# Gate units between state input units, the state gate's tile in another slot, and a state group inside the branch product

## The chip, the cores and the metric

The kernel runs on one core of one Trainium2 chip. The metric is the device time of one execution in microseconds (us). Three runs of the kernel before gave 1543.25, 1544.30 and 1544.58 us; the median is 1544.3 us.

## The reference, cut to what matters

Two layers, each a feed-forward block, a token mixer and a second feed-forward block, on 256 tokens of width 1024, all in float32. Only the mixer is touched.

```python
u = rms_norm(h, mix_norm[l])
z_s, xbc, dt_s, qkv, z_d, b_d, a_d, gate_s, gate_d = split(u @ w_in[l])
y_s = mamba2_branch(z_s, xbc, dt_s, ...)      # causal conv + silu, state-space recurrence, norm per group
y_d = deltanet_branch(qkv, z_d, b_d, a_d, ...) # conv + silu, gated delta rule, norm per head
merged = sigmoid(gate_s) * (y_s @ ssm_w_branch[l]) + sigmoid(gate_d) * (y_d @ dn_w_branch[l])
h = h + merged @ w_out[l]
```

The state branch (`mamba2_branch`) has four groups of eight heads. For each group the inputs `xs` (512 channels) go through a convolution of four taps and silu; a decay matrix of 128x128 per head and chunk of 128 tokens weighs them; the result is gated by `silu(z_s)` and normalised per group.

## The kernel before, in words

All large products run on TensorE (PE) as three products of split operands: every float32 weight tile of 128x1024 is loaded as `wraw`, rounded by ScalarE (ACT) to `whi` (line 68, `prep`), and VectorE (DVE) takes the rest, `wlo = wraw - whi` (line 71). Five raw tiles and five pairs of split tiles are kept (`NRAW`, `NSPL`), so that loads and splits run ahead of the products by five tiles; a split tile comes free when PE has made its last product with it.

The mixer is a list of units, written by hand in `ORDER`, that is gone through once per layer. The units that matter here:

- `x` g i: half of a state group's inputs (`xs_unit`). 48 products of 256 columns with two weight tiles into one PSUM bank, then for each half of the bank the convolution: ACT scales (`ca<-xs`), DVE adds three taps (`ca<-xs,lp,ca`), ACT applies silu into `xsT` (`xsT<-ca`).
- `g` s n p: half of a gate's product (`gate`), for s=0 the state gate and s=1 the delta gate. 24 products of 512 columns with two weight tiles; two halves fill two PSUM banks, and ACT takes tanh of them into the tile `tg` (`tg<-t`).
- `D` g: the decay of group g (`decay`). SyncE's queue (SP) loads 1 MB from DRAM into the tile `dc`; DVE subtracts (`dc<-dc,ac`), limits (`dc<-dc`, line 78), ACT takes exp, DVE multiplies (`dc<-dc,cbt`). Even groups have `dc` in slot `sA`, odd ones in `sB`; a group's load starts when PE has made the last `ydb` product of two groups before.
- `S` g and `T` g: the two halves of `ssd`. `S` transposes `xsT` on PE into two banks `xsb` (eight transposes, four chunks of channels by two halves of the tokens), and DVE makes `xD`, `xdt` and `xe` of them. `T` multiplies with the decay (`ydb`, 32 pairs of products, and `yob`), DVE adds and gates (`xD`, `yo`, `yz`), ACT sums the squares (`jk`), GpSimd (POOL) takes the reciprocal root (`srr`, line 210), and ACT scales (`yz<-yz,srr`).
- `o`, `N`: the delta branch's product (`dn_T`, `dn_branch`): PE transposes a head pair (`oT`), DVE multiplies (`og`), ACT and DVE split it (`bh<-og`, `bl<-og`), then PE makes 24 products `b` of 512 columns per pair, 96 in all, over four PSUM banks.
- `y` and, after the list, `branch("s", 8, ss_T)`: the state branch's product; eight pieces of 24 products `b`, for each of which PE transposes `yz` (`yT`) and ACT and DVE split it (`bh<-yT`, `bl<-yT`) one piece ahead.

The list sets each unit's weights in the order of loading and the order in which tiles and banks are handed out. Within that, a scheduler orders the instructions of each engine; each engine then runs its own list strictly in turn, so an instruction that waits holds up all behind it. PSUM has four banks for products (`accb`) and four for transposes and small products (`trb`), each handed out in turn. A slot such as `sC` holds one tile at a time: first `Q`, then `BC` (the state branch's B and C), which the `cbb` products read for the last time before the first gate unit ends. The state gate's tile `tg` shares `sA` with the decays of groups 0 and 2.

Of the kernel before, what the change touches and what calls it, by code (L numbers as in the profile page):

```python
# [7 lines left out]
F32 = mybir.dt.float32  # L8
# [8 lines left out]
P = 128  # L17
D = 1024
# [26 lines left out]

ORDER = """
z20 s z10 z11 s z21 s M k1 k0 q1 k2 k3 K1 K0 q3 q0 K3 K2 v0 q2 I Q0 I Q3 I z30 v1 z31 Q2 v2 V0 I v3
V1 I V3 I Q1 V2 d0 R R R b3 R b2 b0 R b1 R d2 R x00 R d1 x01 R d3 R R P R g100 g101 D0 S0 x10 T0 D1
x11 g110 g111 S1 x20 T1 o x21 N D2 y S2 D3 x30 x31 T2 g000 g010 g001 S3 g011 T3
""".split()  # L50


# [1 line left out]
def trunk_kernel(ctx, tc, x, wst, wsm, norms, lpar, rpar, cst, out):  # L54
# [5 lines left out]
    slots = ctx.enter_context(tc.tile_pool(name="slots", bufs=1))  # L60
# [6 lines left out]
    def act(o, i, func=AF.Copy, **kw):  # L67
        return A.activation(out=o, in_=i, func=func, **kw)  # L68
# [21 lines left out]
    def accb(name):  # L90
        return accp.tile([P, 512], F32, tag="acc", name=name)
# [9 lines left out]
    def plan_plain(j, n):  # L101
        for i in range(j, j + n):
            stream.append(("w", i))
            plan.append(("d", [len(stream) - 1], len(stream)))
        return j + n

    def plan_ffn(j):


        o, j2, held = j + 4 * FC, j + 4 * FC + 22, []  # L110
        for kind in FFN:
            if kind in "fc":
                j = plan_plain(j, 4 if kind == "f" else 2)
            elif kind == "d":
                o = plan_plain(o, 1)
            elif kind == "A":
                y = len(stream)
                stream.extend([("y", o), ("w", o + 1), ("w", o + 2)])
                plan.append(("q0", (y, y, y + 1), y + 2))
                plan.append(("q1", (y, y + 1, y + 2), y + 3))  # L120
                plan.append(("q2", (y + 1, y, y + 2), y + 3))
                plan.append(("q3", (y, o + 3), y + 3))
                held.append((y, o + 2))
                o += 4
            else:
                y, b22 = held.pop(0)
                stream.append(("w", b22))
                plan.append(("q4", (len(stream) - 1,), len(stream)))
                stream.append(("w", b22 + 1))
                plan.append(("q5", (len(stream) - 1,), len(stream)))  # L130
                plan.append(("q6", (y,), len(stream)))
        return j2

    j0 = 0
    for _ in range(DEPTH):
        j0 = plan_ffn(plan_plain(plan_ffn(j0), mix))
# [259 lines left out]
    def out_chunks(ps, stat, ks, last, group=1, split=False, first=None):  # L396

        for g0 in range(0, len(ks), group):
            kk = ks[g0 : g0 + group]
            ws = [(k, take()) for k in kk]  # L400
            for t in range(2):
                order = [(k, n) for n in range(2) for k in range(len(kk))]
                if t == 1 and not split:
                    m = len(kk) - 2 if len(kk) == NSPL else len(kk)
                    order = [(k, n) for k in range(m) for n in range(2)]
                    order += [(k, n) for n in range(2) for k in range(m, len(kk))]
                order = [(k, n, 0, 512) for k, n in order]
                if t == 1 and split:
                    order = [o for o in order if o[1] == 0]
                    order += [(k, 1, c, c + 256) for c in (0, 256) for k in range(len(kk))]  # L410
                state["sums"] = []
                for k, n, c0, c1 in order:
                    k, (wh, wl) = ws[k]
                    sh, sl = stat(k, t)
                    c = slice(n * 512 + c0, n * 512 + c1)
                    begin = k == 0 if first is None else first and t == n == 1
                    bank = ps[t][n][:, c0:c1]
                    if c0:
                        begin, bank = k == kk[0], ps[2][:, 0:256]
                    ins = mm3(bank, sh, sl, wh[:, c], wl[:, c], begin, k == last)  # L420
                    state["sums"].append(ins)
# [171 lines left out]
    def mixer(l, nxt):  # L593
# [17 lines left out]
        def tok_unit(key, part, done):  # L611

            if part != 1:
                open_[key] = [accb("t0"), accb("t1")]
            tok_chunk(open_[key], range(KT) if part is None else range(4 * part, 4 * part + 4))
            if part != 0:
                for t in range(2):
                    done(t, open_[key][t])

        def z_unit(g, part):  # L620
            if part != 1:
                yz[g] = slots.tile([P, 2, 512], F32, tag=f"y{g}", name="yz")
            tok_unit(("z", g), part, lambda t, ps: act(yz[g][:, t, :], ps[:], AF.Silu))
# [386 lines left out]
        def drain(g):  # L1010
            for _ in g:
                pass
# [15 lines left out]
        def bcm(i):  # L1028
            if "BC" not in late:
                late["BC"] = slots.tile([P, 8, S], F32, tag="sC", name="BC")  # L1030
            bc_unit(i, late["BC"])

        def zdm(i):
            if "zdT" not in late:
                late["zdT"] = slots.tile([P, 8, S], F32, tag="sE", name="zdT")
            zd_unit(i)
# [102 lines left out]
        tg = {}  # L1139

        def gate(s_, n, part):
            if s_ not in tg:
                tg[s_] = slots.tile([P, 2, D], F32, tag=("sA", "sD")[s_], name="tg")
            v = tg[s_][:, :, n * 512 : (n + 1) * 512]
            tok_unit(("g", s_, n), part, lambda t, ps: act(v[:, t, :], ps[:], AF.Tanh, scale=0.5))

# [28 lines left out]
                stt(ol[:, k], bank[:, k * S : (k + 1) * S], w, f(oh[:, k]), ALU.mult, ALU.subtract)  # L1175
            brT[("s", j)] = (oh, ol)

        def branch(kind, n, mk, tail=1):
            ps = [[accb("b"), accb("b")] for _ in range(2)]
            held = {}  # L1180

            def stat(k, t):
                oh, ol = held[k // 2]
                return oh[:, k % 2, t * P : (t + 1) * P], ol[:, k % 2, t * P : (t + 1) * P]

            made = 1
            for j0 in list(range(n - tail)) + [n - tail]:
                js = range(j0, j0 + (tail if j0 == n - tail else 1))
                while made < min(js[-1] + 2, n):
                    mk(made)  # L1190
                    made += 1
                for j in js:
                    held[j] = brT.pop((kind, j))
                out_chunks(ps, stat, [2 * j + i for j in js for i in range(2)], 2 * n - 1, group=2 * len(js))
            return ps

        def dn_branch():
            ps = branch("d", 4, dn_T)
            m = tg[1]
            for t in range(2):  # L1200
                for n in range(2):
                    sl = slice(n * 512, (n + 1) * 512)
                    stt(m[:, t, sl], m[:, t, sl], 1.0, ps[t][n][:], ALU.add, ALU.mult)
# [5 lines left out]
        def step(name):  # L1209
            kind, arg = name[0], name[1:]  # L1210
            num = [int(c) for c in arg if c.isdigit()]
            if kind == "z":
                z_unit(num[0], num[1])
            elif kind in "kqv":
                rests[name] = units[kind](*num)
            elif kind in "KQV":
                drain(rests[name.lower()])
            elif kind == "s":
                next(sc, None)
            elif kind == "M":  # L1220
                masks()
            elif kind == "I":
                next(inv, None)
            elif kind == "R":
                next(rc, None)
            elif kind == "b":
                bcm(*num)
            elif kind == "d":
                zdm(*num)
            elif kind == "x":  # L1230
                xs_unit(*num)
            elif kind == "P":
                drain(ssd_pre())
            elif kind == "D":
                decay(*num)
            elif kind == "g":
                gate(*num)
            elif kind == "S":
                heads[num[0]] = ssd(*num)
                next(heads[num[0]])  # L1240
            elif kind == "T":
                drain(heads[num[0]])
            elif kind == "o":
                dn_T(0)
            elif kind == "y":
                ss_T(0)
            elif kind == "N":
                dn_branch()
# [1 line left out]
        for name in ORDER:  # L1250
            step(name)
        m = tg[1]
        ps = branch("s", 8, ss_T)
        mh = slots.tile([P, KT, S], F32R, tag="sE", name="mh")
        ml = slots.tile([P, KT, S], F32R, tag="sH", name="ml")
        def merge(t):
# [30 lines left out]
    for t in range(2):  # L1287
# [3 lines left out]
        o = tmp2("fo"), tmp2("fo")  # L1291
        for i, (c0, c1) in enumerate(cuts):
            junk = tmp2("junk")
            act(junk[:, : c1 - c0], h[:, t, c0:c1], AF.Square, scale=1.0 / 32.0, accum_out=ss[:, i : i + 1])
            n = c0 // 512
# [143 lines left out]
```

## Time and profile before

| | |
|---|---|
| time, median of three runs | 1544.3 us |
| span of the profiled execution | 1539.7 us |
| median less that span | 4.6 us |
| PE, busy share of the span | 99% |
| DVE | 80% |
| ACT | 61% |
| mixer's part from the first gate unit to the merge, layer 1 and 2 | about 400 to 569 us and 1160 to 1330 us |

The profile is of one execution; of it the span alone is told, and the 4.6 us that it lacks against the median lie before its first and after its last instruction, or are the difference between two executions. The views used below are the page (shares and the chain of waits that ended last), groups of instructions with their mean time, the instructions in order of time, and busy time by stretches. "x24" is a count; a bracket at a row's end tells how long the engine sat idle before it and what ended that.

### The profile page before, as it was taken

How to read it: one execution, taken by the hardware profiler on the slowest of the kernel's cores; microseconds unless marked ns; L12 is line 12 of the kernel's file. 1: busy time of each engine (PE TensorE's matmuls, PEld its weight loads, DVE VectorE, ACT ScalarE, POOL GpSimd, SP SyncE). 2: the span in 40 equal slices, each digit the busy share in tenths (PEclk: the TensorE clock that was granted, in tenths of full speed). 3: DMA queues.
4: the chain of work that ended last, by engine and by line, in shares of the span. 5: the costliest groups of instructions: out<-in, count | busy, mean ns of one | idle time of the engine just before them, and what ended most of it. 6: DMA issues, size and time to landing. Idle time of an engine off the chain costs nothing.

```text
span 1539.7 us, 29072 instructions
## 1 busy us (share of the span) xinstructions
PE 1522.8 (99%) x11473; PEld 1384.4 (90%) x11473; DVE 1229.7 (80%) x1859; ACT 944.8 (61%) x1532; POOL 81.8 (5%) x92
## 2 busy tenths in 40 slices
PE   8999999999999999999999999999999999999998
PEld 7999889999888888999899998899998888899997
DVE  6878769967899766789778887689589996677886
ACT  5655667765665645555555566676756666455565
POOL 0000110000000000000100012010000000000010
PEclk9999999999999999999999999999999999999999
DMA  7687775653565556587867687665345555556785
GB/s 277 190 265 231 226 228 167 187 164 111 178 213 171 163 166 196 185 256 211 261 225 225 208 253 229 197 193 180 117 141 202 179 170 186 176 177 195 247 241 156
DMA packets 98831, 305.73 MB, mean 199 GB/s; under 512 B 22837, under 2 KB 23813, under 8 KB 97670
## 3 DMA queue, kind: packets, MB, share of 16 engines
q1 hardware_dynamic: 93796, 290.95, 57.2%
q0 software_dynamic: 4608, 12.58, 5.1%
q8 instruction: 90, 1.47, 0.4%
q14 instruction: 47, 0.39, 0.1%
q10 hardware_dynamic: 290, 0.33, 0.1%
HBM read 297.72 MB, written 1.92 MB: 195 GB/s over the span
## 4 chain that ended last, share of the span: by engine, by line
PE 89%; DVE 4%; ACT 2%; DMA 2%; issue 1%; SPq 1%; POOL 0%; POOLq 0%; ACTq 0%; DVEq 0%
PE fc L346 10%; PE fc L340 9%; PE fc L345 9%; PE t L366 9%; PE o L337 4%; PE o L335 4%; PE o L336 4%; PE f L366 3%; PE b L335 3%; PE b L337 3%; PE b L336 3%; PE p L336 2%; PE p L337 2%; PE p L335 2%; PE xs L345 1%; PE xs L340 1%
## 5 line engine op out<-in xcount | busy, mean ns | idle before, releaser
L71 DVE TENSOR_TENSOR wlo<-wraw,whi 128x1024 fp32r<-128x1024 f32 x488 | 591.8, 1221 | 186.7 <-ACT whi L68 172.2
L68 ACT ACTIVATE whi<-wraw 128x1024 fp32r<-128x1024 f32 x488 | 511.6, 1059 | 271.0 <-PE fc L345 92.5
L346 PE MATMUL fc<-uW,wlo 128*128 128x256 f32 x1280 | 354.9, 277 | 0.0
L340 PE MATMUL fc<-uW,whi 128*128 128x256 f32 x1280 | 354.1, 277 | 0.0
L345 PE MATMUL fc<-uW,whi 128*128 128x256 f32 x1260 | 348.3, 276 | 0.0
L340 PEld LDWEIGHTS fc<-uW,whi 128*128 128x128 f32 x1280 | 240.5, 188 | 0.8
L346 PEld LDWEIGHTS fc<-uW,wlo 128*128 128x128 f32 x1280 | 240.5, 188 | 0.0
L345 PEld LDWEIGHTS fc<-uW,whi 128*128 128x128 f32 x1260 | 236.5, 188 | 0.8
L366 PE MATMUL t<-whi,uW 128*128 128x512 f32 x512 | 165.3, 397 | 0.0
L366 PEld LDWEIGHTS t<-whi,uW 128*128 128x128 f32 x512 | 95.9, 188 | 21.6 <-issue 1.3
L68 ACT ACTIVATE whi<-wsum 128x1024 fp32r<-128x1024 f32 x64 | 68.0, 1062 | 58.8 <-PE fc L345 32.9
L366 PE MATMUL t<-wlo,uW 128*128 128x512 f32 x256 | 100.2, 392 | 0.0
L71 DVE TENSOR_TENSOR wlo<-wsum,whi 128x1024 fp32r<-128x1024 f32 x64 | 78.2, 1221 | 7.9 <-ACT whi L68 5.6
L335 PE MATMUL b<-whi,bh 128*128 128x512 f32 x192 | 76.1, 398 | 0.3
L336 PE MATMUL b<-wlo,bh 128*128 128x512 f32 x192 | 74.9, 390 | 0.0
L337 PE MATMUL b<-whi,bl 128*128 128x512 f32 x192 | 74.2, 393 | 0.0
L340 PE MATMUL xs<-uW,whi 128*128 128x256 f32 x256 | 72.8, 284 | 0.0
L346 PE MATMUL xs<-uW,wlo 128*128 128x256 f32 x256 | 71.4, 279 | 0.0
L345 PE MATMUL xs<-uW,whi 128*128 128x256 f32 x254 | 70.6, 278 | 0.0
L335 PE MATMUL o<-whi,gh 128*128 128x512 f32 (+1 forms) x160 | 62.0, 388 | 0.0
L337 PE MATMUL o<-whi,gl 128*128 128x512 f32 (+1 forms) x160 | 61.8, 386 | 0.0
L336 PE MATMUL o<-wlo,gh 128*128 128x512 f32 (+1 forms) x160 | 61.7, 386 | 0.0
(337 smaller groups left out, 3291.7 us busy)
## 6 DMA issues: line engine op xcount, KB each, us to landing
wraw<-in_wst_dram SPq DMA_DIRECT2D x504, 512.0 KB, 4.9
wsum<-in_wst_dram SPq DMA_DIRECT2D x16, 512.0 KB, 7.3
wsum<-in_wst_dram POOLq DMA_DIRECT2D x16, 512.0 KB, 8.7
dc<-rdram SPq DMA_DIRECT2D x8, 1024.0 KB, 8.5
nw<-in_norms_dram SPq DMA_DIRECT2D x6, 512.0 KB, 5.9
h<-u POOLq DMA_DIRECT2D x12, 256.0 KB, 6.8
gb<-rdram SPq DMA_DIRECT2D x8, 256.0 KB, 5.6
h<-in_x_dram SPq DMA_DIRECT2D x4, 256.0 KB, 3.7
```

Source lines behind the costliest of these rows:

```text
L68: return A.activation(out=o, in_=i, func=func, **kw)
L71: return V.tensor_tensor(out=o, in0=a, in1=b, op=op)
L335: PE.matmul(ps, lh, rh, start=start, stop=False)
L336: PE.matmul(ps, lh, rl, start=False, stop=False)
L337: return PE.matmul(ps, ll, rh, start=False, stop=stop)
L340: PE.matmul(ps, wh, mh, start=start, stop=False)
L345: PE.matmul(ps, wh, ml, start=False, stop=False)
L346: PE.matmul(ps, wl, mh, start=False, stop=stop)
L366: ins = PE.matmul(ps[t][:], st, mv, start=k0 == 0 and j == 0, stop=k0 == KT - 2 and j == 5)
```

## The change

Three edits of the mixer. In `ORDER` the gate units no longer stand in blocks: one half of a gate unit stands between two `x` units, and the decays `D2` and `D3` and the halves `T1`, `T2` move with them. `S3` and `T3` leave the list and are called inside the state branch's product, before its pieces 1 and 3 (`between`). The state gate's tile moves from slot `sA` to `sC`, so that the first half of that gate can stand before the decay of group 2 has been used.

```diff
@@ ORDER @@
-V1 I V3 I Q1 V2 d0 R R R b3 R b2 b0 R b1 R d2 R x00 R d1 x01 R d3 R R P R g100 g101 D0 S0 x10 T0 D1
-x11 g110 g111 S1 x20 T1 o x21 N D2 y S2 D3 x30 x31 T2 g000 g010 g001 S3 g011 T3
+V1 I V3 I Q1 V2 d0 R R R b3 R b2 b0 R b1 R d2 R x00 R d1 x01 R d3 R R P R g100 D0 g101 S0 x10 T0 D1
+g110 x11 g111 S1 g000 x20 g001 T1 D2 o x21 N y S2 x30 D3 g010 T2 x31 g011
@@ gate @@
-                tg[s_] = slots.tile([P, 2, D], F32, tag=("sA", "sD")[s_], name="tg")
+                tg[s_] = slots.tile([P, 2, D], F32, tag=("sC", "sD")[s_], name="tg")
@@ branch @@
-        def branch(kind, n, mk, tail=1):
+        def branch(kind, n, mk, tail=1, between={}):
...
             for j0 in list(range(n - tail)) + [n - tail]:
                 js = range(j0, j0 + (tail if j0 == n - tail else 1))
+                if j0 in between:
+                    step(between[j0])
                 while made < min(js[-1] + 2, n):
@@ after the list @@
-        ps = branch("s", 8, ss_T)
+        ps = branch("s", 8, ss_T, between={1: "S3", 3: "T3"})
```

The instructions are the same in number on every engine; their order moves. Up to group 0's `ydb` it is the same on PE, DVE, ACT and SP. Three places, the same in both layers:

PE, group 1's transposes `xsb`. Before, six of the eight follow `g111`, and the last two stand 15 products into `x20`:

```order
L340 MATMUL xs<-uW,whi 128x256
L345 MATMUL xs<-uW,whi 128x256
L1101 MATMUL xsb<-cs,xsT 128x128 x2
L346 MATMUL xs<-uW,wlo 128x256
L340 MATMUL xs<-uW,whi 128x256
```

In the change four follow `g111`, two stand seven products into `g000`, and the last two eight products into `x20`:

```order
L342 MATMUL xs<-uW,whi 128x128
L343 MATMUL xs<-uW,whi 128x128
L346 MATMUL xs<-uW,wlo 128x256
L340 MATMUL xs<-uW,whi 128x256
L1101 MATMUL xsb<-cs,xsT 128x128 x2
L345 MATMUL xs<-uW,whi 128x256
```

Both read the `xsT` of `x11`. Between the end of `x11` and the last two there stood `g110`, `g111` and 15 products; now there stand `g111`, `g000` and eight products, and `x11` itself comes 24 products later.

ACT, after group 1's `ydb` (`jk`, `yz`) and at the start of the delta branch's product (`bh<-og`). Before:

```order
L68 ACTIVATE jk,sss<-yz 128x512
L68 ACTIVATE whi<-wraw 128x1024
L68 ACTIVATE jk,sss<-yz 128x512
L68 ACTIVATE ca<-xs,lp 128x256
L68 ACTIVATE bh<-og 128x512
L68 ACTIVATE xsT<-ca 128x256
L68 ACTIVATE yz<-yz,srr 128x512 x2
```

The change:

```order
L68 ACTIVATE xsT<-ca 128x256
L68 ACTIVATE jk,sss<-yz 128x512 x2
L68 ACTIVATE whi<-wraw 128x1024
L68 ACTIVATE yz<-yz,srr 128x512 x2
L68 ACTIVATE bh<-og 128x512
L68 ACTIVATE ca<-xs,lp 128x256
```

The first `bh`, which the branch's first product reads, now stands behind the two `yz` that need POOL's `srr`.

DVE, the same place. Before:

```order
L71 TENSOR_TENSOR yz<-yz,xD 128x512
L74 SCALAR_TENSOR_TENSOR ca<-xs,lp,ca 128x254
L74 SCALAR_TENSOR_TENSOR og<-oT,lp,zdT 128x512
L74 SCALAR_TENSOR_TENSOR ca<-xs,lp,ca 128x253
L79 TENSOR_SCALAR sss<-sss 128x2
L71 TENSOR_TENSOR wlo<-wraw,whi 128x1024
L71 TENSOR_TENSOR bl<-og,bh 128x512
```

The change:

```order
L71 TENSOR_TENSOR yz<-yz,xD 128x512
L74 SCALAR_TENSOR_TENSOR og<-oT,lp,zdT 128x512
L79 TENSOR_SCALAR sss<-sss 128x2
L71 TENSOR_TENSOR dc<-dc,ac 128x2048
L71 TENSOR_TENSOR wlo<-wraw,whi 128x1024
L71 TENSOR_TENSOR bl<-og,bh 128x512
```

The subtraction of group 3's decay, which needs that group's load, now stands before the first `bl`; before, it stood after the fourth `og`. On SP the load of group 3's decay moves behind four more weight tiles.

## The prediction, on record before the changed kernel ran

> **What bounds the kernel now.** I read the page's shares first, then the chain of waits, then the stretches of the first layer's mixer.
>
> ```profile
> PE 1522.8 (99%) x11473; PEld 1384.4 (90%) x11473; DVE 1229.7 (80%) x1859; ACT 944.8 (61%) x1532; POOL 81.8 (5%) x92
> PE 89%; DVE 4%; ACT 2%; DMA 2%; issue 1%; SPq 1%; POOL 0%; POOLq 0%; ACTq 0%; DVEq 0%
> core 0: us, PE busy (x) PEld busy (x) DVE busy (x) ACT busy (x) POOL busy (x), PEclk, DMA share, GB/s
> 424.30:459.40 35.10, 34.06 (x283) 30.64 (x281) 34.40 (x51) 24.89 (x38) 2.35 (x2) 1.00 0.68 221
> 459.40:482.20 22.80, 22.76 (x103) 18.70 (x104) 21.58 (x27) 12.63 (x17) 0.87 (x1) 1.00 0.46 138
> 482.20:523.30 41.10, 41.10 (x345) 35.40 (x344) 36.33 (x50) 26.28 (x36) 1.60 (x1) 1.00 0.56 187
> 523.30:569.00 45.70, 45.70 (x216) 37.62 (x215) 28.16 (x38) 23.39 (x35) 0.70 (x1) 1.00 0.53 170
> ```
>
> PE is busy 99% of the span, at a clock of 1.00 in these stretches. No product is removed, so the change can win only the time in which PE waits. The four stretches show where that is: from group 0's `ydb` to the delta branch's product, 35.10 us of which DVE works 34.40, PE lacks 1.04 us; in the other three it lacks 0.04 us at most. DVE is full at the front (34.40 of 35.10) and loose at the back (28.16 of 45.70); the change moves gate products, which ask little of DVE, forward, and group 3's work back. Its aim is the 1.04 us. A busy PE may still run below its pace, so I looked at starts in order of time:
>
> ```profile
> 497.13 16.54 PE t L366 x72
> 385.55 0.28 PE L340 MATMUL xs<-uW,whi 128*128 128x256 f32 x1
> 385.66 0.28 PE L345 MATMUL xs<-uW,whi 128*128 128x256 f32 x1
> 443.38 0.28 PE L345 MATMUL xs<-uW,whi 128*128 128x256 f32 x1
> 444.59 0.44 PE L1101 MATMUL xsb<-cs,xsT 128*128 128x128 f32 x2 [0.93 <-ACT xsT L68]
> 1205.95 0.33 PE L1101 MATMUL xsb<-cs,xsT 128*128 128x128 f32 x1 [0.94 <-ACT xsT L68]
> 458.25 1.04 PE L1154 MATMUL oT<-cs,vb 128*128 128x128 f32 x8
> 459.44 0.50 PE L335 MATMUL b<-whi,bh 128*128 128x512 f32 x1
> ```
>
> A product of 512 columns takes 16.54/72 = 0.23 us, so 24 take 5.5; one of 256 columns about 0.115 us, so a unit of 48 takes 5.6. Starts further apart than that, where the change works, are two in each layer: 1.1 us (443.38 to 444.59, less one product) before group 1's last two transposes, which wait for `xsT`; and about 0.4 us before the delta branch's first product, for `bh`. That is all that can be won: 1.5 us a layer, 3.0 us in all, 0.19% of 1544.3. A change of 0.2%, 3.1 us, is about what a measurement of this kernel tells from none.
>
> **The change part by part.** PE's work is the same; the transposes stand in other pieces. Group 1's are in three pieces instead of two, but `oT` loses one (ten and two become twelve) and group 3's stand next to `yT`. The two transposes at 444.59 held PE for 0.2 us beyond the wait, so one piece less is worth about 0.1 us a layer; bounds 0 to 0.2.
>
> *Group 1's last transposes (gain).* They need the second half of `x11` through the convolution. In the change `x11` runs after `g110` (5.5 us later, ends at about 435.8), then come `g111` to 441.2, six transposes and `g000` to 447.7, eight products to 448.7. On ACT stand before that `xsT`: two tanh, which wait for `g111` (441.4), `whi`, `xsT` and `ca`, then group 2's exp between two table loads.
>
> ```profile
> 453.71 1.28 ACT L68 ACT_TABLE_LOAD   x1
> 455.01 0.42 ACT L68 ACTIVATE xsT<-ca 128x256 f32<-128x256 f32 x1
> L68 ACT ACTIVATE dc<-dc 128x2048 f32<-128x2048 f32 x8 | 15.3, 1916 | 0.1
> L68 ACT ACTIVATE whi<-wraw 128x1024 fp32r<-128x1024 f32 x488 | 511.6, 1059 | 271.0 <-PE fc L345 92.5 <-DMA wraw<-in_wst_dram 29.1 <-PE b L337 27.7
> ```
>
> From 441.4: 0.5 (tanh) + 1.0 (`whi`) + 0.4 + 0.5 (`xsT`, `ca`) + 1.3 + 1.9 + 1.3 + 0.4 = 7.3, so `xsT` is there at 448.7, when PE is. The wait of 1.1 falls to about 0.2: 0.9 us won a layer. There is no slack in it: 1 us late on ACT and nothing is won. Bounds 0 to 1.1.
>
> By the Trainium skill ("ScalarE: Activation LUTs", section "What ACT_TABLE_LOAD costs") each switch of tables costs a load of about 1.28 us and a drain of about 1.38 more. The rows agree with the first and not with the second: the load of 453.71 is followed by `xsT` 1.30 us later. By the page's whole price the two loads ahead of `xsT` would put it 2.8 us later, an estimate from its figures.
>
> *The delta branch's first product (loss).* Take S for the start of group 1's `ydb`.
>
> ```profile
> 449.04 2.02 PE ydb L1115 x64
> 456.32 0.68 DVE L71 TENSOR_TENSOR yz<-yz,xD 128x512 f32<-128x512 f32 x1
> 458.41 0.17 DVE L79 TENSOR_SCALAR sss<-sss 128x2 f32<-128x2 f32 x1
> 458.66 1.61 POOL L210 TENSOR_TENSOR srr<-sss,mhalf 128x2 f32<-128x2 f32 x1 [25.77 <-DVE sss L79]
> 458.76 0.62 ACT L68 ACTIVATE bh<-og 128x512 fp32r<-128x512 f32 x1
> 460.30 1.34 ACT L68 ACTIVATE yz<-yz,srr 128x512 f32<-128x512 f32 x2 [0.61 <-POOL srr L210]
> ```
>
> Before, `bh` went at S+9.7, ahead of `yz`. In the change the convolution of `x20` has run through by then (`g001` lies between), so the last `yz` product on DVE is about 1.2 us earlier (S+6.1 for S+7.3) and `sss` comes at S+7.7. But `bh` now stands behind both `yz`, which stand behind POOL: S+7.7, 0.25 to POOL's start, 1.61, then 1.34, then 0.62 for `bh` itself: S+11.5. PE is there at S+10.35 (before, 459.08 = S+10.05 without its wait, and two transposes more ahead). PE waits 1.15 us where it waited 0.4: 0.75 us lost a layer. Behind `bh` on ACT wait the `ca` of `x21` and the next `whi`, both with room. Bounds: 0.4 won (POOL's result in time) to 1.2 lost.
>
> *Group 3's decay (a load in front of the first `bl`).* Its load cannot start before group 1's `ydb` has ended:
>
> ```profile
> 451.09 0.33 SPq L1061 DMA_DIRECT2D dc<-rdram  x1
> DMA to landing us min/median/max: 6.2/8.5/10.6
> 470.05 2.28 DVE L71 TENSOR_TENSOR dc<-dc,ac 128x2048 f32<-128x2048 f32 x1
> L71 DVE TENSOR_TENSOR wlo<-wraw,whi 128x1024 fp32r<-128x1024 f32 x488 | 591.8, 1221 | 186.7 <-ACT whi L68 172.2 <-PE wb L891 4.0
> 459.63 0.68 DVE L71 TENSOR_TENSOR bl<-og,bh 128x512 fp32r<-128x512 f32 x1
> ```
>
> Issued at S+2.1 it lands at S+8.3 to S+12.7; DVE wanted it at S+21 before and reaches it at S+7.8 now. Behind it stand one `wlo` and the first `bl`: 2.25 + 1.15 + 0.65 = 4.05 us from landing to the end of `bl`. PE can make six products with `bh` alone (1.4 us), so it needs `bl` at S+12.9, and the load must land by S+8.85, 6.7 us after its issue. The load of 451.09 took 6.5 us, the one in its place in layer 2 6.2. I take that, as there too one weight tile was under way beside it: nothing lost. Bounds 0 to 1.8 (the median of 8.5), and 3.9 at the maximum.
>
> *Group 3 in the state branch.* `S3` adds five operations of 0.6 us to DVE and `T3` six, in a stretch of 45.70 us where DVE has 17.5 us free; PE's pieces last 5.9 us each and the splits run five tiles ahead. What stands closest:
>
> ```profile
> 529.24 0.48 PE L335 MATMUL b<-whi,bh 128*128 128x512 f32 x1
> 529.26 0.46 ACT L68 ACTIVATE bh<-yT,lp 128x256 fp32r<-128x256 f32 x1
> 529.75 0.48 DVE L74 SCALAR_TENSOR_TENSOR bl<-yT,lp,bh 128x256 fp32r<-128x256 f32 x1 [1.93 <-ACT bh L68]
> 530.49 0.40 PE L337 MATMUL b<-whi,bl 128*128 128x512 f32 x1
> ```
>
> The piece after `T3` had its second `bl` ready at 530.23 and used it at 530.49, before; the same sequence now falls at piece 4, with one `wlo` less in between. Nothing lost; up to 0.5 if the 0.26 us go. The fourth bank of the branch comes free with the convolution of `x31`, now one gate half (5.5 us) before the branch instead of four (both halves of `g00`, of `g01`): I put the last tap about 4 us after `g011` and PE's first use there too, 0.1 us lost, bounds 0 to 0.5. If either cover goes, PE stands still for as long.
>
> *Slot.* `sC` is free when `g000` comes (its `cbb` readers end by about 405, `g000` starts at 441), so the tile makes no wait: 0.
>
> Sum for a layer: -0.1 - 0.9 + 0.75 + 0 + 0 + 0.1 = -0.15 us; two layers, -0.3 us. The profiled span goes from 1539.7 to 1539.4; the runs lay 4.6 us above that span, and I keep that: 1544.3 - 0.3 = **1544.0 us**, no change that can be told.
>
> **Rivals.**
> 1. *All waits go.* For it: two gate halves move in ahead of the delta branch, 11 us of PE with 4.9 us of splits for DVE. Against: group 3's subtraction now needs a load before S+8.85, and `bh` stands behind POOL. 2 x (1.1 + 0.4 + 0.1) = 3.2: 1541.1 us.
> 2. *Slower: the decay's load holds DVE in front of the first `bl`.* One mechanism, at the start of the delta branch's product: it decides from 6.7 us between issue and landing on. For it: the median of the eight such loads is 8.5. Against: the two at this place took 6.5 and 6.2. At 8.5 us 1.8 us a layer, with the sum above 2 x 1.65 = 3.3: 1547.6 us; at the maximum of 10.6, 1552.
> 3. *Table switches on the way to `xsT`.* Two loads and exp now stand before group 1's last `xsT`, where before they came after it. Were each switch to hold ACT as long again as its load (1.28 us), `xsT` would come 2.6 us later and PE wait for it: 2 x (2.6 - 0.15) = 4.9, 1549.2 us. Against: 1.30 us from load to next start in the trace. (This is the page's rule named above, with its price of a switch; by the page's own drain it is 2.8 for 2.6.)
>
> That the change does not do what it says is not among them: the order on PE and DVE shows the units moved.
>
> **How the numbers follow.** Forecast 0.74; rival 1 0.07; rival 2 0.16; rival 3 0.03. Rival 1 ends at the edge of 3.1 us, so faster takes 0.05 of it and 0.01 from the forecast's own spread; slower takes rivals 2 and 3 and 0.02 of the spread, 0.21. The forecast's own range, 1541.8 to 1546.8, holds one of its terms at its bound per layer (a loss of 1.2 for 0.75, or `xsT` late by 1). The range reaches up to rival 2's price and some of its tail: 1541.2 to 1548.6 us.
>
> **What would show it.** Right: PE's wait before group 1's last transposes under 0.5 us, released by ACT `xsT`; before the first `b` a wait of about 1 us released by ACT `bh`, with `yz` before it waiting for POOL; group 3's `dc<-dc,ac` within 1 us after its load's landing at about S+8.5. In the state branch no start later than its pace. Wrong: a wait of DVE for `dc` over 1 us and PE waiting for `bl`; PE idle in the branch before piece 1, 4 or 6; any stretch outside the mixer that moves.

## The result and the profile after

The changed kernel takes 1546.22 us (median of 18 runs, 1544.04 to 1551.44), the kernel before 1543.22 us on the same chips (18 runs, 1541.56 to 1544.79): a ratio of 1.0022, with a 95% interval of 1.0015 to 1.0029. On another chip, in the fourth experiment below, it was 1.0013 (1.0004 to 1.0022). The change makes the kernel about 2 to 3 us slower; the forecast was no change, 1544.0 us. The profiled execution took 1545.48 us with a span of 1543.7, 4.0 us over the span before.

The page of the changed kernel, its shares and its chain of waits:

```profile
PE 1524.5 (99%) x11473; PEld 1384.4 (90%) x11473; DVE 1230.9 (80%) x1859; ACT 945.1 (61%) x1532; POOL 78.2 (5%) x92
PE 89%; DVE 3%; DMA 3%; ACT 3%; issue 2%; SPq 1%; POOL 0%; POOLq 0%; ACTq 0%
```

Nothing shows there: the sums are nearly those of before. What moved stands in the view of PE's waits over one mixer (engine, line, what it waited for: us in total, times, longest). First the kernel before, the row before the fourth `cbb` in the first and the second layer (the ones for `xsb` <- `xsT`, 0.9 us each, are the two that the prediction showed in the timeline):

```profile
PE cbb L1045 <- DVE vb L71: 0.6, 1, 0.6
...
PE cbb L1045 <- DVE vb L71: 1.3, 1, 1.3
```

The same view of the changed kernel, first and second layer:

```profile
PE b L337 <- DVE bl L71: 1.0, 1, 1.0
PE cbb L1045 <- DVE vb L71: 0.9, 1, 0.9
PE b L335 <- ACT bh L68: 0.3, 1, 0.3
...
PE cbb L1045 <- DVE vb L71: 1.9, 1, 1.9
PE b L337 <- DVE bl L71: 1.3, 1, 1.3
PE b L335 <- ACT bh L68: 0.3, 1, 0.3
```

The wait for `xsT`, 0.9 us a layer, is gone, as forecast. In its place stands a wait for the first `bl` of the delta branch, 1.0 and 1.3 us. The view counts from the modelled end of the product before; by starts, as the prediction counts, each wait is about 0.2 us longer. The rows of the timeline in the first layer, and of the two starts in the second:

```profile
461.79 0.33 SPq L1061 DMA_DIRECT2D dc<-rdram  x1
467.40 0.17 DVE L79 TENSOR_SCALAR sss<-sss 128x2 f32<-128x2 f32 x1
467.65 0.69 POOL L210 TENSOR_TENSOR srr<-sss,mhalf 128x2 f32<-128x2 f32 x1 [34.30 <-DVE sss L79]
468.38 1.34 ACT L68 ACTIVATE yz<-yz,srr 128x512 f32<-128x512 f32 x2
468.88 2.29 DVE L71 TENSOR_TENSOR dc<-dc,ac 128x2048 f32<-128x2048 f32 x1 [1.31 <-DMA dc<-rdram]
469.62 0.62 ACT L68 ACTIVATE bh<-og 128x512 fp32r<-128x512 f32 x1
470.29 0.51 PE L335 MATMUL b<-whi,bh 128*128 128x512 f32 x1 [0.27 <-ACT bh L68]
...
471.58 0.39 PE L336 MATMUL b<-wlo,bh 128*128 128x512 f32 x1
472.23 0.68 DVE L71 TENSOR_TENSOR bl<-og,bh 128x512 fp32r<-128x512 f32 x1
472.97 0.50 PE L337 MATMUL b<-whi,bl 128*128 128x512 f32 x1 [1.00 <-DVE bl L71]
...
1232.65 2.29 DVE L71 TENSOR_TENSOR dc<-dc,ac 128x2048 f32<-128x2048 f32 x1 [1.58 <-DMA dc<-rdram]
1235.07 0.39 PE L336 MATMUL b<-wlo,bh 128*128 128x512 f32 x1
1236.73 0.50 PE L337 MATMUL b<-whi,bl 128*128 128x512 f32 x1 [1.27 <-DVE bl L71]
```

Group 3's decay load was issued at 461.79 and landed at 468.86, 7.07 us later. DVE stood idle for it for 1.31 us, then came the subtraction, one `wlo` and `bl`. PE made its six products with `bh` and waited from 471.81 (471.58 + 0.23) to 472.97: 1.16 us; in the second layer 1236.73 - 1235.07 - 0.23 = 1.43. This is the second rival of the prediction. But POOL's `srr` took 0.69 us and not 1.61, so `bh` was there at 470.2 and PE lost only 0.49 us ahead of it (0.36 before).

The waits before the fourth `cbb` (0.6 and 1.3 before, 0.9 and 1.9 after) lie ahead of all that the change moves, on a stretch with the same order in both kernels. They come back below, since they vary between executions by as much as the whole effect.

### The profile page after: what moved, and what is told of

Same layout as the page of the kernel before. It is cut to its first block, busy times and chain, and to the rows that moved or that the text cites. A ratio compares the mean times of both kernels' runs of the same rounds, so it can differ in the third digit from the quotient of the medians.

```text
span 1543.7 us, 29056 instructions
## 1 busy us (share of the span) xinstructions
PE 1524.5 (99%) x11473; PEld 1384.4 (90%) x11473; DVE 1230.9 (80%) x1859; ACT 945.1 (61%) x1532; POOL 78.2 (5%) x92
## 3 DMA queue, kind: packets, MB, share of 16 engines
HBM read 297.72 MB, written 1.92 MB: 194 GB/s over the span
## 4 chain that ended last, share of the span: by engine, by line
PE 89%; DVE 3%; DMA 3%; ACT 3%; issue 2%; SPq 1%; POOL 0%; POOLq 0%; ACTq 0%
PE t L366 10%; PE fc L346 9%; PE fc L340 9%; PE fc L345 9%; PE o L337 4%; PE o L335 4%; PE o L336 4%; PE f L366 3%; PE b L337 3%; PE b L335 3%; PE b L336 3%; DMA dc<-rdram 2%; PE p L336 2%; PE p L337 2%; PE p L335 2%
```

## The experiments

All were compared with the kernel before on the same chip. The lists of waits are the view shown above, of the first layer unless said otherwise.

**1. Group 3's subtraction behind the last `og`.** The one edit to the changed kernel:

```
+    with tc.issue_after(last_og):        # group 3 only
         tt(dc, dc, ac..., ALU.subtract)
```

> The changed kernel with one edit: group 3's subtraction (dc<-dc,ac) may issue on DVE only behind the last og of the delta branch, so the first bl no longer stands behind the decay's load. Theory (the load holds DVE, DVE holds bl, PE waits 1.16 and 1.43 us for it): PE's wait before the first b<-whi,bl goes to under 0.2 us in both layers, the time falls by about 2.6 us against the changed kernel, to about 1543.6 us, ratio to the kernel before 0.999 to 1.001. Rival (bh behind the yz scaling): bl still stands behind bh, nothing changes, ratio 1.002. Rival (group 3's work inside the state branch): nothing changes before that branch, ratio 1.002. Rival (the new order of gate and state input units as such): ratio 1.002.

Measured: 1542.95 us, ratio 0.9996 (0.9987 to 1.0005). The load took 7.08 us, as before the edit. PE's waits in the branch and ahead of it (0.5 for 0.6 in the second layer):

```profile
PE cbb L1046 <- DVE vb L71: 0.6, 1, 0.6
...
PE b L335 <- ACT bh L68: 0.3, 1, 0.3
```

The wait for `bl` is gone and the time with it: 2.3 us under the changed kernel on the same chip (1545.25, the fourth). The units, the slot and the state branch's groups stand as in the change, so what the change loses hangs on the place of this subtraction. With it the rest of group 3's decay (minimum, exp and multiply) comes later too, and PE takes the first `bl` products earlier in its list. Whether the loss comes through the load that the subtraction waits for, or through its own 2.29 us, this run doesn't say: it takes both away.

**2. `bh` ahead of group 1's `yz` on ACT.**

```
     rsqrt(rr, ss)
+    yield                                # after sss and srr
     for t in range(2): act(yv, yv, scale=rr[:, t])
 ...
 elif kind == "o":
     dn_T(0)
+    with tc.issue_after(first_bh): drain(heads[1])
```

> The changed kernel with one edit: on ACT the two yz scalings of group 1 stand behind the first bh instead of ahead of it. Theory (decay's load): PE's wait before the first b (0.49 us) goes to about 0.1, but it gains nothing, since the first bl still comes when the decay's load has landed and PE's wait there grows by what the first b gained; time as the changed kernel's within 0.4 us, ratio to the kernel before 1.002. Rival (bh behind yz is what costs): the time falls by 1 us or more, ratio 1.0015 or lower.

Measured: 1545.26 us, ratio 1.0011 (1.0002 to 1.002), the changed kernel's time (1545.25). PE's wait in the branch, first layer:

```profile
PE b L337 <- DVE bl L71: 1.2, 1, 1.2
```

The wait for `bh` is gone, the one for `bl` is 0.1 to 0.2 us longer, and the time is the same. The edit moved more than ACT: the scheduler put one `wlo` behind the first `bl` on DVE, and eight of the twelve `oT` ahead of the first product behind it on PE, so that PE and `bl` both come more than 1 us earlier after group 1's `ydb`. No gain from an earlier `bh` can be told while the decay's load holds `bl`.

**3. The kernel before, with group 3's decay early.**

```
-x11 g110 g111 S1 x20 T1 o x21 N D2 y S2 D3 x30 ...
+x11 g110 g111 S1 x20 T1 D3 o x21 N D2 y S2 x30 ...
```

> The kernel before with one edit: group 3's decay stands directly behind the end of group 1 in the list, so that its subtraction, which needs a load that cannot start before group 1's ydb has ended, stands on DVE ahead of the delta branch's first og and bl. None of the change's other edits is in it. Theory (decay's load holds DVE): a new wait of DVE for dc and of PE in the delta branch's first piece, 1 to 4 us a layer (og is held too, so bh as well), time 2 to 8 us over the kernel before, ratio 1.0013 to 1.005. Rivals (bh behind yz; group 3 in the state branch; the new order of the units): none of these is in this kernel, ratio 1.000.

Measured: 1561.52 us, ratio 1.0115 (1.0101 to 1.0129): 18 us, far more than any theory gave. It doesn't bear out the load:

```profile
459.11 2.29 DVE L71 TENSOR_TENSOR dc<-dc,ac 128x2048 f32<-128x2048 f32 x1 [0.19 <-DMA dc<-rdram]
...
464.93 1.28 ACT L68 ACT_TABLE_LOAD   x1
466.22 1.91 ACT L68 ACTIVATE dc<-dc 128x2048 f32<-128x2048 f32 x1
468.04 0.61 ACT L68 ACTIVATE bh<-og 128x512 fp32r<-128x512 f32 x1
468.70 0.80 PE L335 MATMUL b<-whi,bh 128*128 128x512 f32 x1 [4.34 <-ACT bh L68]
```

The load (6.46 us) landed as DVE came to it. With the decay that early the scheduler also put its minimum on DVE ahead of `og`, and its table load and exp on ACT ahead of the first `bh`. PE waited for `bh`. The kernel shows how dear this place is for anything else, and tells nothing on the load.

**4. The changed kernel once more**, on the chip of the first three.

> The changed kernel itself, on the same chip and in the same rounds as the other three, so that their differences against it can be read. Ratio to the kernel before 1.002 (1.0015 to 1.0029 the first time). In its profile PE's wait for the first bl, 1.16 and 1.43 us the first time, comes again at 0.8 to 1.8 us a layer if it is the decay's load, which took 7.1 to 7.3 us there and decides from 6.7 us.

Measured: 1545.25 us, ratio 1.0013 (1.0004 to 1.0022). The waits, first layer and second:

```profile
PE cbb L1045 <- DVE vb L71: 1.8, 1, 1.8
PE b L337 <- DVE bl L71: 0.8, 1, 0.8
...
PE cbb L1045 <- DVE vb L71: 1.9, 1, 1.9
PE b L337 <- DVE bl L71: 1.4, 1, 1.4
```

The wait for `bl` came again; here the load took 6.81 us in the first layer, and DVE waited 1.07. The wait before `cbb` tripled against the profile before (0.6), in a stretch where nothing differs.

**5. The first two edits together.**

> Both edits in the changed kernel: group 3's subtraction behind the last og on DVE, and group 1's yz scalings behind the first bh on ACT. Theory (the decay's load gates the first bl, and bh behind yz is the next wait, 0.49 us a layer, which counts only once the load is out of the way): PE's waits before the first b and the first bl are both under 0.15 us, the time is 0.8 us under that of the kernel with the first edit alone (2 x 0.4), ratio to the kernel before 0.9985 to 0.9998. If the first bh gains nothing even so: the same ratio as that kernel, 0.9996.

Measured: 1542.6 us, ratio 0.9997 (0.9988 to 1.0006). On PE eight `oT` move as in the second. No wait is left in the branch, but the 0.8 us against the first experiment can't be told: in the second layer of its profile PE waited 2.4 us before `cbb`, where it was 0.5 in the first experiment's. A gain of that size is below what these runs tell apart.

**6. Group 3 out of the state branch again.**

```
-x30 D3 g010 T2 x31 g011
+x30 D3 x31 T2 g010 S3 g011 T3            # and no between in branch("s", ...)
```

> The changed kernel with its part for the state branch undone: S3 and T3 stand in the list again, T3 ahead of the branch, x31 ahead of T2; all else as changed, the decay's load included. The prediction's term for group 3 in the state branch (0, and 0.1 us for the bank of x31): the ratio stays at 1.0013 to 1.002, PE's wait for the first bl stays at 0.9 to 1.6 us. Rival (group 3's work in the branch costs what the change lost): ratio back to 1.000.

Measured: 1544.83 us, ratio 1.0009 (1.0000 to 1.0018), with the wait for `bl` in place:

```profile
PE b L337 <- DVE bl L71: 1.2, 1, 1.2
```

Undoing this part leaves the wait. The time alone decides little: the interval touches 1.0000 and overlaps the changed kernel's, so a cost of some tenths of a us, as the prediction had for the bank of `x31`, is not excluded.

**9. The decay's load ahead of a weight load.** In the changed kernel three weight loads of 0.5 MB had been issued in the 6 us ahead of the decay's; the edit puts the last of them behind it on SP's queue, and leaves the order of every other engine (a tie behind the first `og`, not shown in the cut, keeps the subtraction in its place):

```
+    T1 L3 D2 ...                          # L3: group 3's load alone
+    if state.get("decay"):                # in load(): the next weight tile
+        behind.enter_context(tc.issue_after(state.pop("decay").ins))
```

> The changed kernel with one edit: on SP's queue the weight load that stood just ahead of group 3's decay load stands behind it; the order on PE, DVE, ACT and POOL is the changed kernel's, group 3's subtraction ahead of the first bl included. In the changed kernel three weight loads of 0.5 MB were issued in the 6 us ahead of the decay's (456.08, 457.65, 460.74 us, against 461.79) and it took 7.07 us; in the kernel before one was, and it took 6.46. Theory (the first bl waits for the subtraction because the load lands late, and the load is late for the weight loads in flight): the load takes 5.5 to 6.4 us, DVE's wait for it goes from 1.3 to under 0.5 us, PE's wait for the first bl from 1.2 to 1.6 us to 0.2 to 0.7, time 1 to 2 us under the changed kernel's, ratio 1.0000 to 1.001. Rival (it is the subtraction's own 2.3 us on DVE ahead of bl, not the load): PE's wait stays over 1 us, ratio 1.0013 to 1.002.

Measured: 1547.15 us, ratio 1.0026 (1.0016 to 1.0036): not better. In the first layer the load was as late as ever (issued 463.08, DVE started at 470.12), with the weight load issued right behind it. In the second it took 5.3 us (1226.43 to 1231.73), and that layer is the telling one:

```profile
470.12 2.29 DVE L71 TENSOR_TENSOR dc<-dc,ac 128x2048 f32<-128x2048 f32 x1 [1.24 <-DMA dc<-rdram]
...
1232.12 2.29 DVE L71 TENSOR_TENSOR dc<-dc,ac 128x2048 f32<-128x2048 f32 x1
1232.30 2.67 POOL L212 TENSOR_TENSOR srr<-sss,mhalf 128x2 f32<-128x2 f32 x1 [34.49 <-DVE sss L79]
1236.91 0.50 PE L337 MATMUL b<-whi,bh 128*128 128x512 f32 x1 [2.24 <-ACT bh L68]
```

DVE didn't wait for the load, and PE lost more than ever. The subtraction ran at once, just ahead of POOL's `srr`, which took 2.67 us for the 0.69 of the changed kernel; `yz` and `bh` stood behind it. The theory of the load alone fell here.

**12. Half of the load.** To see that apart from the weight loads, group 3's load was cut to 0.5 MB, with the orders of PE, DVE and ACT as in the changed kernel (the same tie as in the ninth; on POOL a memset of 0.95 us comes in, done 4.9 us ahead of `srr`). The decay of the group's other four heads is left out of the computation:

```
+    n = 4 if g == 3 else 8
-    dma_start(dc[:], rdram[8 * g : 8 * g + 8]...)
+    dma_start(dc[:, 0:n], rdram[8 * g : 8 * g + n]...)
+    if n < 8: G.memset(dc[:, n:8], 0.0)
```

> The changed kernel with group 3's decay load cut to its first four heads (0.5 MB for 1 MB; the other four heads are set to zero on POOL, so that half of group 3's decay is left out of the computation). The order on PE, DVE, ACT and SP is the changed kernel's: the subtraction of 2.29 us still stands ahead of the first bl. Theory (it is the landing of the load): the load takes 5 to 6 us instead of 7.0, DVE's wait for it (1.07 to 1.71 us in the profiles of the changed kernel) is under 0.4 us, PE's wait for the first bl (0.94 to 1.58 us, 0.13 to 0.15 us under DVE's wait each time) goes under 0.25 us, and the time falls by about 2 us to that of the kernel before, ratio 0.9995 to 1.0008. Rival (the subtraction's own 2.29 us of DVE ahead of bl): PE's wait stays over 0.9 us, ratio 1.0013 to 1.002.

Measured: 1547.4 us, ratio 1.0024 (1.0012 to 1.0035). Both the theory and its rival missed: the wait for `bl` went, the time didn't fall.

```profile
467.15 2.29 DVE L71 TENSOR_TENSOR dc<-dc,ac 128x2048 f32<-128x2048 f32 x1
467.32 2.68 POOL L210 TENSOR_TENSOR srr<-sss,mhalf 128x2 f32<-128x2 f32 x1 [4.88 <-DVE sss L79]
470.03 1.33 ACT L68 ACTIVATE yz<-yz,srr 128x512 f32<-128x512 f32 x2 [2.03 <-POOL srr L210]
471.27 0.61 ACT L68 ACTIVATE bh<-og 128x512 fp32r<-128x512 f32 x1
471.94 0.50 PE L335 MATMUL b<-whi,bh 128*128 128x512 f32 x1 [2.25 <-ACT bh L68]
```

The load took 5.51 us and DVE didn't wait. The subtraction held POOL's `srr`, that held `yz`, `yz` held `bh`, and PE waited 2.47 us (by starts) ahead of the first `b`, 2.61 in the second layer, where the changed kernel loses 0.49 + 1.16 and 0.49 + 1.43.

**13. Half of the load, and `bh` ahead of `yz`** (the edits of the twelfth and the second).

> The kernel of the twelfth experiment (half of group 3's decay load, so half of its decay left out; orders of the engines as changed) with the edit of the second: group 1's yz scalings behind the first bh on ACT. In the twelfth PE waited 2.47 and 2.61 us for the first bh, which stood behind yz and so behind POOL's srr, 2.68 and 2.83 us long there against 0.69 in the changed kernel, while DVE ran the subtraction of 2.29 us. Theory (DVE's subtraction holds POOL's srr, srr holds yz, yz holds bh): srr stays at 2.7 us, but bh no longer stands behind it, so PE's wait before the first b goes under 0.2 us, the first bl (not held by the load either) under 0.3, and the time falls by 4 to 5 us against the twelfth, ratio 0.9990 to 1.0005. Rival (bh is late by itself, or its og is): PE's wait before the first b stays over 1.5 us, ratio 1.002.

Measured: 1543.0 us, ratio 1.0002 (0.9993 to 1.0011).

```profile
469.07 2.68 POOL L210 TENSOR_TENSOR srr<-sss,mhalf 128x2 f32<-128x2 f32 x1 [4.88 <-DVE sss L79]
469.65 0.61 ACT L68 ACTIVATE bh<-og 128x512 fp32r<-128x512 f32 x1
470.32 0.49 PE L335 MATMUL b<-whi,bh 128*128 128x512 f32 x1
471.78 1.34 ACT L68 ACTIVATE yz<-yz,srr 128x512 f32<-128x512 f32 x2 [1.51 <-POOL srr L210]
```

`srr` is as long as in the twelfth, but `bh` no longer stands behind it: neither the first `b` nor the first `bl` waits. With that the chain from DVE's subtraction over POOL to `bh` is shown. That `bl` doesn't wait either owes something to the scheduler, which here, as in the second, put the `wlo` of 1.22 us behind it.

**7, 8, 10 and 11. The wait before the fourth `cbb`.** It has the same form: on DVE `vb` and the `cbm` multiplies stand behind group 0's subtraction, which waits for its load. Four kernels tried to win it.

```
 7 (before):  subtractions of groups 0 and 1 behind the last cbm multiply
10 (before):  group 1's decay load six weight loads later
 8 (changed): as 7, with the edits of 1 and 2
11 (changed): as 10, with the edits of 1 and 2
```

> The kernel before with one edit: the subtractions of groups 0 and 1 may issue on DVE only behind the last cbm multiply, so that the cbm multiplies and with them the banks of cbb no longer stand behind a decay's load. It tests the same mechanism at its other place, which both kernels have: PE's wait before the fourth cbb, 0.85 and 1.53 us before (0.79 to 2.14 in the runs so far, with a load of 8.5 to 11.3 us). Theory: that wait goes, 2.0 to 2.4 us, ratio 0.9985. Against it: DVE is busy 34.40 of 35.10 us from group 0's ydb on, and the subtraction that comes later may be late for group 0's ydb; then the wait stands there instead and the ratio is 1.000.

> The changed kernel with all three edits: group 3's subtraction behind the last og, group 1's yz scalings behind the first bh, the subtractions of groups 0 and 1 behind the last cbm multiply. If the waits add up: 1545.3 - 2.6 (first bl) - 0.8 (first bh) - 2.2 to 4 (fourth cbb, 2.07 and 2.14 us in the second profile of the changed kernel) = 1538 to 1540 us, ratio to the kernel before 0.9965 to 0.998. If the front's wait only moves to group 0's ydb: 1542, ratio 0.999.

> The kernel before with one edit: group 1's decay load, which is issued 1.5 us after group 0's, is issued six weight loads later; its subtraction then stands on DVE behind group 0's ydb. Group 0's load lands after 8 to 9 us, with 1 MB of group 1's behind it in the same queue. Theory (the transfers in flight share the 16 DMA engines, so the second load delays the first): group 0's load lands 1 us or more earlier, PE's wait before the fourth cbb goes from 0.85 to 2.1 us to under 0.4, and the time falls by 1 to 2.5 us if nothing is late for it later, ratio 0.9985 to 0.9995. Rival (the load is served in order, the second does not touch the first): the wait stays, ratio 1.000.

> The changed kernel with group 3's subtraction behind the last og, group 1's yz scalings behind the first bh, and group 1's decay load six weight loads later: the fifth experiment (ratio 0.9997) with the edit of the tenth. If the front's wait goes in both layers (0.28 and 2.68 us in the fifth experiment's profile): 1.5 to 3 us under the kernel before, ratio 0.998 to 0.999, faster than both kernels. If the second load does not delay the first: 0.9997.

Measured: the seventh 1544.28 us, ratio 1.0007 (0.9998 to 1.0017); the eighth 1548.07, 1.0032 (1.0020 to 1.0044); the tenth 1543.02, 0.9995 (0.9986 to 1.0004); the eleventh 1551.41, 1.0053 (1.0040 to 1.0066). Where the wait went, a row or more of each in the order 7, 8, 10, 11 (PE's waits, for the eighth also POOL, ACT and DVE, for the eleventh POOL):

```profile
PE xsb L1105 <- ACT xsT L68: 1.3, 1, 1.3
...
PE xsb L1105 <- ACT xsT L68: 3.0, 1, 3.0
434.66 4.94 POOL L210 TENSOR_TENSOR srr<-sss,mhalf 128x2 f32<-128x2 f32 x1 [27.71 <-DVE sss L79]
439.63 1.34 ACT L68 ACTIVATE yz<-yz,srr 128x512 f32<-128x512 f32 x2 [4.62 <-POOL srr L210]
441.95 1.23 DVE L71 TENSOR_TENSOR wlo<-wraw,whi 128x1024 fp32r<-128x1024 f32 x1 [2.91 <-ACT whi L68]
...
PE cbb L1045 <- DVE vb L71: 0.6, 1, 0.6
...
PE t L366 <- ACT whi L68: 2.6, 1, 2.6
PE cbb L1046 <- DVE vb L71: 1.2, 1, 1.2
437.33 8.28 POOL L210 TENSOR_TENSOR srr<-sss,mhalf 128x2 f32<-128x2 f32 x1 [27.35 <-DVE sss L79]
```

In the seventh and eighth the wait for `cbb` is gone, and a longer one for `xsT` stands later in the same stretch, where DVE had 0.7 us to spare before (the prediction's 34.40 of 35.10 us); what delays `xsT` in the seventh was not followed further. In the eighth the rows show the chain of the twelfth at another place: two `wlo` and group 2's subtraction ran one after another on DVE (434.48 to 439.04), group 0's `srr` took 4.94 us, `yz` and the `whi` behind it waited on ACT, DVE then waited for `whi`, and the last tap ahead of `xsT` came late. In the tenth the wait for `cbb` stayed (0.6 and 1.6 us): group 1's load, which in the first layer follows 1.5 us behind, is not what makes group 0's late. In the eleventh five operations ran in a row on DVE (two `wlo` and three of the decays, 437.16 to 445.06), group 0's `srr` took 8.28 us in both layers, and PE waited for the `whi` behind it, 2.6 us in the first layer and 1.0 in the second. No run takes this chain apart in the eighth and eleventh; it is read from their rows. None is told faster than the kernel before.

## Why the prediction was wrong

**The step that failed** is the term for group 3's decay: "I take that [6.5 us] ... nothing lost. Bounds 0 to 1.8". It was 1.16 and 1.43 us in the two layers, 0.94 and 1.58 in the second profile. Two things were wrong in it.

First the duration. The loads in that place took 6.5 and 6.2 us before, with one weight load issued 0.6 us ahead and the one before that 5.9 us ahead. In the changed kernel the three last ones were issued 5.7, 4.1 and 1.1 us ahead, of which the second landed 1.7 us after the decay's issue, and the decay's load took 7.07, 6.81, 7.08 and 7.03 us in the first layer of the changed kernel, its repeat, the first and the second experiment. The move of the gate units forward also moved their weight tiles' loads, and the step looked at the queue's order only, not at what is in flight. That the weight loads cause the difference is an argument, not shown. For it: in the seventh experiment the last weight load stood 5.7 us ahead in both layers, and the decay's took 4.7 and 4.5 us. Against: taking the last one from ahead of it in the ninth left the load at 7.0 us in one layer and gave 5.3 in the other.

Second, and more, the term was not independent of the one before it. The limit of 6.7 us was worked out for a PE that is held until S+11.5 by `bh`. With DVE idle in wait for the load, POOL's `srr` ran in 0.69 us, `bh` came 0.9 us earlier and PE asked for `bl` about 0.75 us earlier (S+12.15 for S+12.9, S being the start of group 1's `ydb`): the limit was then 467.72 - 461.79 = 5.9 us (PE wants `bl` at 471.81, 1.16 us before it starts; so the landing would have to be 1.16 us ahead of DVE's start at 468.88). And a load that has landed when DVE comes to the subtraction lets it start ahead of `srr`, which makes `bh` late:

| kernel, layer | DVE waits for the load | `srr` | PE waits for `bh` | for `bl` | together |
|---|---|---|---|---|---|
| changed, 1 | 1.31 | 0.69 | 0.49 | 1.16 | 1.65 |
| changed, 2 | 1.58 | 0.70 | 0.49 | 1.43 | 1.92 |
| ninth, 1 | 1.24 | 0.70 | 0.49 | 1.12 | 1.61 |
| ninth, 2 | 0 | 2.67 | 2.46 | 0 | 2.46 |
| twelfth, 1 | 0 | 2.68 | 2.47 | 0 | 2.47 |
| twelfth, 2 | 0 | 2.83 | 2.61 | 0 | 2.61 |
| first (subtraction later), 1 | - | 0.70 | 0.49 | 0 | 0.49 |
| before, 1 | - | 1.61 | 0.36 | 0 | 0.36 |

Late or early, with the subtraction in that place and `bh` behind `yz` one of the two waits stood in every layer measured. Where DVE waits for the load, PE's wait for `bl` is 0.12 to 0.15 us less than DVE's, in each of these rows.

**Point by point.** *Group 1's last transposes*: right; the wait went from 1.09 to 0.29 and 0.30 us (0.2 forecast), with `xsT` done at 449.07 (448.65 + 0.42; 448.7 forecast). *Table switches* (third rival): out. In the changed kernel's timeline the second load is followed 1.30 us after its start, as the first is (444.12, exp at 445.42):

```profile
447.35 1.28 ACT L68 ACT_TABLE_LOAD   x1
448.65 0.42 ACT L68 ACTIVATE xsT<-ca 128x256 f32<-128x256 f32 x1
```

The drain that the Trainium skill gives ("ScalarE: Activation LUTs", "What ACT_TABLE_LOAD costs") on top of the load doesn't show here either.

*The delta branch's first product*: the order was right, `bh` behind `yz` behind `srr`, and `sss` came at S+7.74 (S = 459.66; S+7.7 forecast). The size was wrong: 0.13 us lost for 0.75, through `srr`, 0.69 us for the 1.61 taken from a row in which DVE had run a `wlo` beside it. *Group 3 in the state branch*: no new wait in the view; undoing it changed nothing that can be told. *Bank of `x31`*: the starts of the branch's first piece lie 0.16 us further behind their pace than before (0.25 for 0.09), 0.1 forecast. *Slot*: no wait at `g000` shows.

**The sum.** By starts and for both layers: transposes -1.6, first `b` +0.3, first `bl` +2.6, first piece of the branch +0.3: +1.6 us, where the forecast's terms gave -0.3. Of the 4.0 us between the two profiled spans another 0.95 is the `cbb` wait, 0.34 + 0.61 us longer in this pair; the remaining 1.4 isn't placed. Where both are on record, the time lies 1.7 to 1.9 us above the span; so the span of 1539.7 before stands for about 1541.5 us (an estimate from these), at the low end of that kernel's 18 runs, and the two spans lie further apart than the medians. Over all profiles the `cbb` wait runs from 0.28 to 2.68 us in kernels that the edits do not touch there, and those of the kernel before and of the changed one don't part. The medians' 1.9 to 3.0 us stand beside it. Without the failed term the forecast can't be told from what was measured: the kernel of the first experiment has everything but that, and lies at 0.9996 (0.9987 to 1.0005), against 0.9998 forecast.

The second rival had the mechanism at 0.16, priced at 1.65 us a layer. The rows spoke for more than that: the two loads quoted as counter-evidence had 0.2 and 0.5 us to spare, and DVE issues in order, so the term could only cost. The median of 8.5 us says less: of the eight loads that view has a landing for six, and the four longer ones stand at other places.

## What to carry to other kernels

An instruction that waits for a load holds all that is queued behind it on its engine: when a change moves it ahead of the operand that the bottleneck needs next, count its landing against that, with the loads that the change itself puts in flight. Two waits that hang on one instruction are one term, not two; work out what each does when the other goes. A short operation's duration is read from rows with the same neighbour: here 0.69, 1.61 and 2.68 us for the same `srr`.

## What the runs showed of the hardware

POOL's `srr`, an operation on 128x2 elements, took 0.69 or 0.70 us where DVE was idle, waited, or ran an operation that reads PSUM (`ca`, `og`, the state branch's `bl`); 1.60 to 1.69 where DVE had begun a `wlo` of 1.22 us shortly before it, or in the third experiment a minimum `dc<-dc` of 1.22; and 2.67 to 2.83 where it was the subtraction of 2.29 us. In the rows of the twelfth experiment it ends 0.56 us after DVE's operation (467.32 + 2.68 against 467.15 + 2.29): it doesn't run beside it, it waits. The Trainium skill ("SBUF — State Buffer", "SBUF: two separate sides") says so: VectorE and GpSimd share a pair of ports, an operation of DVE with two inputs in SBUF that starts first takes it for its whole length against a GpSimd operation that reads SBUF, and "the other fully blocks". The subtraction and `wlo` are such operations; the rows agree.

The wait can be longer than one operation. In the eighth and eleventh experiment, where three and five operations followed one another on DVE, `srr` took 4.94 and 8.28 us and ended 0.56 and 0.55 us after the last of them. In the twelfth the `wlo` that followed the subtraction did not hold it so; what makes the difference no run here shows.

What remains open is why the decay loads vary so much: 4.5 to 11.7 us for the same 1 MB. A part of it the rows show. All above 9.4 us were issued 0.5 to 2.6 us behind another group's: group 1's took 9.3 and 10.6 us in the kernel before, behind group 0's, and 6.3 us in both layers of the tenth, where none stood shortly ahead of it; there group 2's, now 2.6 us behind it, took 10.3 and 9.6 us for 8.5 before. What decides for the others, among them group 3's, neither the load behind (tenth) nor one weight load ahead (ninth) settles.
